# Attention sigmoids kept in PSUM, two kinds of stores moved to SyncE, and a planner that knows of VectorE and GpSimd meeting in SBUF

## The chip, the cores and the metric

The kernel runs on one core of one Trainium2 chip. Such a core has five engines that run side by side, each with its own queue of instructions in fixed order: TensorE (PE in the profile) for matmuls and transposes, VectorE (DVE), ScalarE (ACT), GpSimd (POOL), and SyncE (SP), which here only issues DMAs. They meet through semaphores. Data lies in HBM, in the on-chip memory SBUF, or in PSUM, where TensorE writes its results.

The metric is the device time of one execution in microseconds (us), as the median of several runs. Lower is better. The three runs of the kernel before took 2428.45, 2426.36 and 2428.19 us, median 2428.19.

## The reference

One layer of a decoder, with 2048 tokens of width 1024, all in float32:

```python
a = rmsnorm(x) * g_pre_mix
u = a @ W_in                  # conv value 512, conv gate 512, q 512, k 512, v 512
conv = silu(layernorm(causal_depthwise_conv31(val * sigmoid(gate)) + b))
attn = rmsnorm_per_head(stick_breaking(q, k, v))      # 8 heads of 64
h = x + rmsnorm(concat(conv, attn) @ W_out)
f = (silu(n @ W_gate) * (n @ W_up)) @ W_down          # n = rmsnorm(h), inner width 2816
out = h + rmsnorm(f)
```

Stick-breaking attention has no softmax. With z = q.k / 8, token t gives key s (s < t) the weight sigmoid(z_ts) times the product of 1 - sigmoid(z_tj) over the keys j between s and t. Since 1 - sigmoid(z) = sigmoid(-z), the products are a running product of sigmoid(-z) from the newest key to the oldest.

## The kernel before, in words

**Number format.** A float32 operand is split into a high part H, rounded by ScalarE's copy, and a rest L, made by a subtraction on VectorE or GpSimd. Three matmuls (L x H, H x H, H x L) make one product. The tokens are cut into four groups of 512, and almost every matmul has 512 columns.

**The mixer** is the first half. For each group of tokens it has the input projection (`inproj`, L598 to L602), the convolution on VectorE as 31 taps on a PSUM tile (`taps`, L824), the attention (`attn`) and the output projection (`outproj`, L1041 to L1043). Attention goes head by head (8), chunk by chunk of 512 keys from the newest to the oldest, and in four steps of 128 queries in each. One step of `scores` is: two matmuls write the tile `z` in PSUM (L908, L909; the tile has two buffers), ScalarE writes the sigmoid into an SBUF tile `om` (L911; eight buffers), and VectorE scans `om` in place, from right to left (L914 or L916). A scan is a running product. A diagonal chunk (L914; 128, 256, 384 or 512 wide) adds the mask `lower` and multiplies on; any other chunk (L916, 512 wide) multiplies only, and its second operand does no arithmetic: it is one element of `z`, repeated, except in the later four heads of the last group (`late`), where it is the SBUF constant `one`. There are 320 steps: 128 diagonal ones, 144 with `z` as the operand and 48 with `one`. `values` then transposes the weights (L934), splits them (TH on ScalarE at L590, TL on VectorE at L591) and multiplies them with V (L939, L940). TensorE's results of the input projection go to two PSUM banks (`bank`): for the value columns VectorE multiplies with `sg`, the sigmoid of the gate (L768, L773); for v there are four transposes (L786), whose result is split into two tiles `vt`.

**The feed-forward part** is the second half: a seven-product scheme after Strassen and Winograd. Sums of weight blocks are made on GpSimd ahead of time, in the mixer's shadow (`sums`, L1189). Two steps of it also run beside the mixer: `c11` (88 results) and `p4` (22), each 128x512, which ScalarE copies from PSUM (L1146, L1175) and which are stored in HBM by a DMA that ScalarE itself issues (L1111). `five` computes the other products of the up and gate projections (`b` at L1105; weights split at L1394 and L1395), and the end of the function computes the down projection (`dps` at L1105; operands split at L1622 to L1625, results scaled and added at L1635 and L1654).

**The order.** All instructions are first written in one plausible order, by a list of stages (`PLAN`) and due times. Then `Graph` takes them all, makes the dependencies, and lays them out in time by a list scheduler: `forward` runs a model of the five queues, in which `cost` prices every instruction (busy time, and the later moment at which its result can be used), DMAs have constant prices (`ISSUE`, `LAND`), and buffers are handed out as they come free; `backward` makes the priorities from the reversed program. `arrange` does this 12 times and keeps the order with the earliest end, by the model. `in_order` then ties every engine's instructions in that order. So the order on the chip is fixed when the program is built, and `cost` shapes all of it. On SP, too, a DMA that waits holds up those behind it.

In `cost`, a VectorE operation has one price if an operand is in PSUM and a longer one if all are in SBUF: for 512 elements, with n = 512, a scan 2.04 n + 125 or + 240 ns, a scalar_tensor_tensor 1.04 n + 108 or + 370, a tensor_tensor 1.04 n + 60 or + 500. GpSimd's two-operand operations cost 2.36 n + 125 (products 2.0 n + 125). What the two engines do at the same moment has no bearing on either.

Of the kernel before, what the change touches and what calls it, by code (L numbers as in the profile page):

```python
# [19 lines left out]
P = 128  # L20
# [5 lines left out]
NH = 8  # L26
# [128 lines left out]
def width(a):  # L155
    n = 1
    for _, c in a.ap[1:]:
        n *= int(c)
    return n
# [33 lines left out]
def cost(i, kind, eng, ins, outs):  # L193

    n = width(outs[0])
    if kind == "InstMatmult":
        if size_of(ins[0].dtype) == 4 and not str(ins[0].dtype).endswith("r"):
            return 109, 270
        b = max(width(ins[0]) * 0.443, 109)
        return b, b + 165  # L200
    src = [place(a) for a in ins]
    if eng == "Activation":
        b = n * 0.833 + (49 if src[0] == "PSUM" else 94) + (93 if len(ins) > 1 else 0)
        return b, b + 115
    near = "PSUM" in src or place(outs[0]) == "PSUM"
    if eng == "DVE":
        if kind == "InstTensorScalarPtr":
            if i.is_tensor_tensor_scan:
                b = 2.04 * n + (125 if near else 240)
            elif i.is_scalar_tensor_tensor:  # L210
                b = 1.04 * n + (108 if near else 370)
            else:
                b = 1.04 * n + 160 if place(outs[0]) == "PSUM" else 0.73 * n + 113
        elif kind == "InstBNStatsAggregate":
            b = 93
        elif kind in ("InstTensorReduce", "InstBNStats"):
            b = 1.04 * width(ins[0]) + 48
        elif kind == "InstTensorTensor":
            b = 1.04 * n + (60 if near else 500)
        else:  # L220
            b = n + 100
        return b, b + 100
    if kind == "InstTensorTensor":
        b = 426 + 148 * n if n < 16 else (2.0 if "mult" in str(i.op) else 2.36) * n + 125
    else:
        b = 172 if n == 1 else 280
    return b, b + 65


class Op:  # L230
    def __init__(self, n, ins, eng, dma, busy, late, size):
        self.n, self.ins, self.eng, self.dma = n, ins, eng, dma
        self.busy, self.late, self.size = busy, late, size
        self.after, self.behind, self.tiles = set(), set(), set()


class Graph:


    def __init__(self, insts):  # L240
        self.ops, self.root, self.order, self.users = [], {}, {}, {}
        seen = {}
        for i in insts:
            kind = type(i).__name__
            ins = [a for a in i.ins if hasattr(a, "bass_ap")]
            outs = [a for a in i.outs if hasattr(a, "bass_ap")]
            if not outs:
                continue
            eng, dma = str(i.engine).split(".")[-1], kind == "InstDMACopy"
            busy, late = (ISSUE, 0) if dma else cost(i, kind, eng, ins, outs)  # L250
            o = Op(len(self.ops), i, eng, dma, busy, late, width(outs[0]) * int(outs[0].ap[0][1]) * 4)
            uses = [(a.bass_ap.tensor, box(a), place(a), w) for aps, w in ((ins, False), (outs, True)) for a in aps
                    if hasattr(a.bass_ap.tensor, "tag_meta")]
            for t, b, sp, w in uses:
                if sp != "DRAM" and t.name not in o.tiles:
                    o.tiles.add(t.name)
                    self.users.setdefault(t.name, []).append(o.n)
                    if t.name not in self.root:
                        self.root[t.name] = t
                        self.order.setdefault(t.tag, []).append(t.name)  # L260
                writes, reads = seen.setdefault(t.name, ([], []))
                for old, lst in ((True, writes), (False, reads if w else ())):
                    for q, c, wrote in lst:
                        if sp == "PSUM" or meet(b, c):
                            same = q.eng == eng and not q.dma
                            (o.behind if same and (eng == "PE" or not (old and wrote)) else o.after).add(q.n)
            for t, b, sp, w in uses:
                writes, reads = seen[t.name]
                if sp == "PSUM":
                    writes[:] = [e for e in writes if e[0].eng != eng] + [(o, b, w)]  # L270
                elif w:
                    writes[:] = [e for e in writes if not holds(b, e[1])] + [(o, b, True)]
                    reads[:] = [e for e in reads if not holds(b, e[1])]
                else:
                    reads.append((o, b, False))
            o.behind -= o.after
            self.ops.append(o)
# [32 lines left out]
    def forward(self, ops, prio, slots=True):  # L310
# [18 lines left out]
        busy = dict.fromkeys(ready, 0.0)  # L329
        start, stop = [None] * len(ops), [0.0] * len(ops)  # L330
        moved, flight = 0.0, []
        ev = [(0.0, 0, 0, ())]
        for o in ops:
            if not need[o.n]:
# [28 lines left out]
        while ev:  # L363
# [24 lines left out]
            while look:  # L388
# [5 lines left out]
                while ready[e]:  # L394
# [14 lines left out]
                        moved = max(t + AHEAD, moved) + o.size / RATE  # L409
                        stop[n] = moved + LAND  # L410
                    else:
                        stop[n] = t + o.late
                    heapq.heappush(ev, (busy[e], 1, n, tuple(iss[n])))
                    for lag, then in fin[n].items():
                        heapq.heappush(ev, (stop[n] + lag, 2, n, tuple(then)))
# [8 lines left out]
    def backward(self, start, stop, came):  # L424

        N = len(self.ops)
        rev = [Op(N - 1 - o.n, None, o.eng, o.dma, o.busy, o.late, o.size) for o in self.ops]
        for o in self.ops:
            for p in o.after:
                rev[p].after.add(N - 1 - o.n)  # L430
# [49 lines left out]
def layer_kernel(ctx: ExitStack, tc: tile.TileContext, x, xT, g_pre_mix, w_in, conv_w, conv_b, ln_g, ln_b,  # L480
# [398 lines left out]
    def attn(g):  # L879
# [20 lines left out]
        def scores(u, j):  # L900
# [2 lines left out]
            w = (j + 1) * P if diag else G  # L903
            K = u["K"]
            z = pp.tile([P, G], F32, tag="z", name="z")
            late = g == NG - 1 and u["h"] >= NH // 2
            js = slice(j * P, (j + 1) * P)
            nc.tensor.matmul(z[:, 0:w], hd_["QL"][:, js], K[:, 0:w], start=True, stop=False)  # L908
            nc.tensor.matmul(z[:, 0:w], hd_["QH"][:, js], K[:, 0:w], start=False, stop=True)  # L909
            om = ap.tile([P, G], F32, tag="om", name="om", bufs=NOM)  # L910
            nc.scalar.activation(om[:, 0:w], z[:, 0:w], AF.Sigmoid, scale=-0.125)  # L911
            r = om[:, 0:w][:, ::-1]
            if diag:
                nc.vector.tensor_tensor_scan(r, lower[:, G - w:G][:, ::-1], r, hd_["prev"][j], ALU.add, ALU.mult)  # L914
            else:
                nc.vector.tensor_tensor_scan(r, r, (one if late else z[:, 0:1]).to_broadcast([P, w]), hd_["prev"][j],  # L916
                                             ALU.mult, ALU.bypass)
            hd_["prev"][j] = om[:, 0:1]
            if w == P and g:
                hd_["prev"][j] = sp.tile([P, 1], F32, tag="pv", name="pv", bufs=2)  # L920
# [185 lines left out]

    stored = {}

    def store(t, *key, eng=nc.sync):
        stored[key] = dp.tile([P, *t.shape[1:]], F32, name="_".join(str(k) for k in key))  # L1110
        eng.dma_start(stored[key], t)  # L1111

    def part(t, k, n, *key, eng=nc.sync):

        if key not in stored:
            stored[key] = dp.tile([P, n, G], F32, name="_".join(str(k) for k in key))
        eng.dma_start(stored[key][:, k, :], t)

    fx = {}

# [9 lines left out]
    def c11(g):  # L1130
# [5 lines left out]
        for j in range(HF):  # L1136
            ws = [wts.next() for _ in W]
            pss = [bank("c11") for _ in W]
            for hf in range(2):
                for i, ((WH, WL), ps) in enumerate(zip(ws, pss)):  # L1140
# [3 lines left out]
                            matmul(ps, a[:, kc], b[hf][:, k, :], start=hf == k == 0 and a is WL, stop=last)  # L1144
                    c = next(cs)
                    nc.scalar.activation(c, ps, AF.Copy)  # L1146
                    store(c, "c11", g, i, j, hf, eng=nc.scalar)
                    yield 0.5

    def sums_split(HL, k, t, eng=nc.gpsimd):  # L1150
# [10 lines left out]
    def p4(g):  # L1161
# [4 lines left out]
        for j in range(HF):  # L1166
            for i in range(2):
# [5 lines left out]
                        matmul(ps, a[:, kc], b[0][:, k, :], start=k == 0 and a is WL, stop=last)  # L1173
                c = ev("p4")
                nc.scalar.activation(c, ps, AF.Copy)  # L1175
                store(c, "p4", g, i, j, eng=nc.scalar)
                yield 1

    def sums():
# [609 lines left out]
```

## Time and profile before

| | |
|---|---|
| median of three runs | 2428.19 us (2426.36 to 2428.45) |
| the profiled execution | 2422.51 us, of which its span (first to last instruction) 2420.7 us |
| TensorE busy | 2352.3 us, 97% |
| VectorE busy | 1788.4 us, 74% |
| GpSimd busy | 1207.5 us, 50% |
| ScalarE busy | 1166.5 us, 48% |
| DMA | 656.66 MB, mean 271 GB/s |

All views below are of that one execution, and times in them count from the start of its span. A line of a group reads: line of the code, engine, operation, output<-inputs by the program's names, sizes, count | busy us in all, mean ns of one | us that the engine was idle just before such instructions, and who ended most of it. A line of the waits reads: who waited <- for whom: us in total, times, longest us. A line of the timeline reads: start us, duration us, engine, line, operation, output<-inputs, count, with the idle time before it and who ended it in brackets. A line of a stretch gives each engine's busy us with its count of instructions, then the clock granted to TensorE (1.00 is full), the busy share of the DMA engines and GB/s. PEld is TensorE's loading of weights, which runs beside its matmuls; SPq and ACTq are DMA issues on the queues of SyncE and ScalarE.

### The profile page before, as it was taken

Reading aid. Unit: us, or ns where it says so; the run is one execution under the profiler, and the core shown is the slowest. Engines: PE = TensorE matmul, PEld = TensorE weight load, DVE = VectorE, ACT = ScalarE, POOL = GpSimd, SP = SyncE. Lnnn points to the kernel's source line nnn. Section 1 sums busy time; section 2 is a strip of 40 time slices with the busy share of each in tenths; the row PEclk is TensorE's granted clock in tenths of the full one; section 3 lists DMA queues with packets and bytes.
Section 4 is the critical chain, followed back from the end, with each engine's and each line's share of the span. In section 5 each row is a group of like instructions: output and inputs, shape, how many; then the busy total and the mean of one; then the engine's idle time right before and its main releaser. Section 6 shows DMA issues by size and latency. Waiting matters only on the chain. (4 is left out here: it accounts for less than half of the span.)

```text
span 2420.7 us, 33652 instructions
## 1 busy us (share of the span) xinstructions
PE 2352.3 (97%) x11156; PEld 1929.5 (80%) x11156; DVE 1788.4 (74%) x2177; ACT 1166.5 (48%) x2078; POOL 1207.5 (50%) x994
## 2 busy tenths in 40 slices
PE   7999999999999999999999999999999999999997
PEld 5778887788787878888788887878888888887886
DVE  6997899899998799956842267888766664567556
ACT  4346555474655555455555554334322335454543
POOL 5463235522425234436620047678886445477556
PEclk9999999999999999999999999999999999999998
DMA  9889887897788899987798767999998667658664
GB/s 313 273 260 322 260 252 233 275 317 250 249 276 303 272 308 323 332 292 254 261 316 295 255 233 276 309 311 319 348 336 299 198 236 232 199 189 324 193 193 163
DMA packets 283789, 656.66 MB, mean 271 GB/s; under 512 B 34912, under 2 KB 35424, under 8 KB 283616
## 3 DMA queue, kind: packets, MB, share of 16 engines
q1 hardware_dynamic: 267776, 625.68, 77.6%
q10 hardware_dynamic: 15840, 28.84, 3.1%
q8 instruction: 88, 1.44, 0.2%
q14 instruction: 85, 0.70, 0.1%
HBM read 460.40 MB, written 193.99 MB: 270 GB/s over the span
## 5 line engine op out<-in xcount | busy, mean ns | idle before, releaser
L824 DVE SCALAR_TENSOR_TENSOR cv<-glu,cw,cv 128x512 f32<-128x512 f32 x464 | 345.9, 746 | 6.4
L1395 POOL TENSOR_TENSOR wL<-raw,wH 128x512 fp32r<-128x512 f32 x176 | 264.9, 1529 | 169.9 <-ACT wH L1394 169.7
L1625 DVE TENSOR_TENSOR xL__20078<-t__20080,xH__20077 128x512 fp32r<-128x512 f32 x154 | 197.5, 1288 | 150.3 <-ACT xH__20077 L1624 148.9
L1623 POOL TENSOR_TENSOR xL__20076<-t__20079,xH__20075 128x512 fp32r<-128x512 f32 x154 | 212.5, 1385 | 159.4 <-ACT xH__20075 L1622 155.2
L591 DVE TENSOR_TENSOR TL<-at,TH 128x512 fp32r<-128x512 f32 (+1 forms) x320 | 188.6, 597 | 132.8 <-ACT TH L590 126.7
L598 PE MATMUL inps<-xH,wL 128*128 128x512 f32 x640 | 259.7, 407 | 12.4 <-ACT sg L768 11.7
L602 PE MATMUL inps<-xL,wH 128*128 128x512 f32 x640 | 255.3, 400 | 0.5 <-DVE xL L738 0.5
L600 PE MATMUL inps<-xH,wH 128*128 128x512 f32 x640 | 255.7, 400 | 0.0
L1105 PE MATMUL dps<-xH__20075,xL__20078 128*128 128x512 f32 x616 | 241.6, 392 | 5.6 <-DVE xL__20078 L1625 5.6
L1105 PE MATMUL dps<-xH__20075,xH__20077 128*128 128x512 f32 x616 | 240.8, 391 | 0.0
L1105 PE MATMUL dps<-xL__20076,xH__20077 128*128 128x512 f32 x616 | 239.4, 391 | 0.0
L590 ACT ACTIVATE TH<-at 128x512 fp32r<-128x512 f32 (+1 forms) x320 | 168.8, 536 | 122.8 <-PE at L934 114.2
L552 ACT ACTIVATE wH<-raw 128x1024 fp32r<-128x1024 f32 x156 | 165.8, 1063 | 127.6 <-PE inps L602 57.0
L911 ACT ACTIVATE om<-z 128x512 f32<-128x512 f32 (+2 forms) x320 | 168.4, 540 | 88.9 <-PE z L909 87.3
L556 POOL TENSOR_TENSOR wL<-raw,wH 128x1024 fp32r<-128x1024 f32 x50 | 122.1, 2443 | 163.7 <-ACT wH L552 149.4
L934 PE MATMUL at<-idr,om 128*128 128x128 f32 x1088 | 184.2, 273 | 6.0 <-DVE om L914 3.0
L1622 ACT ACTIVATE xH__20075<-t__20079 128x512 fp32r<-128x512 f32 x154 | 97.1, 630 | 192.7 <-POOL xL__20076 L1623 141.5
L1189 POOL TENSOR_TENSOR sum<-sum 128x512 f32<-128x512 f32 x88 | 126.7, 1440 | 117.9 <-DMA sum<-in_w_up_dram 45.0
L1394 ACT ACTIVATE wH<-raw 128x512 fp32r<-128x512 f32 x176 | 101.4, 624 | 155.9 <-PE b L1105 58.3
L934 PEld LDWEIGHTS at<-idr,om 128*128 128x128 f32 x1088 | 137.1, 140 | 46.2 <-DVE om L914 5.8
L916 DVE TENSOR_TENSOR_SCAN om<-om,z 128x512 f32<-128x512 f32 x124 | 156.8, 1268 | 3.9 <-ACT om L911 3.7
L598 PEld LDWEIGHTS inps<-xH,wL 128*128 128x128 f32 x640 | 121.5, 190 | 37.8 <-ACT sg L768 8.3
(296 smaller groups left out, 6120.7 us busy)
## 6 DMA issues: line engine op xcount, KB each, us to landing
wL<-wL SPq DMA_DIRECT2D x156, 512.0 KB, 5.3
raw<-in_w_in_dram SPq DMA_DIRECT2D x80, 512.0 KB, 6.0
t__20080<-u SPq DMA_DIRECT2D x154, 256.0 KB, 3.0
c<-c ACTq DMA_DIRECT2D x88, 256.0 KB, 5.4
t__20079<-wd SPq DMA_DIRECT2D x88, 256.0 KB, 2.6
K<-kd SPq DMA_DIRECT2D x80, 256.0 KB, 4.9
V<-vd SPq DMA_DIRECT2D x80, 256.0 KB, 4.6
u<-accf SPq DMA_DIRECT2D x22, 768.0 KB, 5.7
```

What stands on the lines that cost most here:

```text
L590: nc.scalar.activation(H, ps, AF.Copy)
L591: nc.vector.tensor_tensor(L, ps, H.bitcast(F32), ALU.subtract)
L598: nc.tensor.matmul(ps, WL[:, kc], aH[t](k), start=k == 0, stop=False)
L600: nc.tensor.matmul(ps, WH[:, kc], aH[t](k), start=False, stop=False)
L602: nc.tensor.matmul(ps, WH[:, kc], aL[t](k), start=False, stop=k == KT - 1)
L824: nc.vector.scalar_tensor_tensor(to, gl[c][:, k:k + G], cw[:, c, k:k + 1], a, ALU.mult, ALU.add)
L911: nc.scalar.activation(om[:, 0:w], z[:, 0:w], AF.Sigmoid, scale=-0.125)
L934: nc.tensor.transpose(pt[:, j * P:(j + 1) * P], u["A"][j][:, b * P:(b + 1) * P], id32)
L1105: return nc.tensor.matmul(ps, a, b, skip_group_check=True, **flags)
L1395: nc.gpsimd.tensor_tensor(l, t, f32(h), sub)
L1623: nc.gpsimd.tensor_tensor(WL, w, f32(WH), sub)
L1625: nc.vector.tensor_tensor(UL, t, f32(UH), sub)
```

## The change

Three things are changed.

1. ScalarE writes the sigmoid back into the PSUM tile `z`; `om` is written by the scan alone. The scan reads `z` from right to left and writes `om`. The second operand of the scans that are not diagonal is always the SBUF constant `one`; the case `late` is gone.
2. The stores of the c11 and p4 results are issued by SP.
3. The planner's prices: VectorE's longer prices for operations with all operands in SBUF are gone. `both_in_sbuf` marks VectorE and GpSimd operations with two inputs at least 128 wide and all operands in SBUF. When, in `forward`, such a VectorE operation starts while a marked GpSimd operation runs, or any GpSimd operation starts while a marked VectorE operation runs, the new one gets longer (`more`) and the running one may (`push`), by shares of what is left of the running one and of the new one's own time. GpSimd's own prices change as well, to 2.35 n + 35 for operations of 16 elements and more.

```diff
@@ cost
-    near = "PSUM" in src or place(outs[0]) == "PSUM"
     if eng == "DVE":
         if kind == "InstTensorScalarPtr":
             if i.is_tensor_tensor_scan:
-                b = 2.04 * n + (125 if near else 240)
+                b = 2.04 * n + 125
             elif i.is_scalar_tensor_tensor:
-                b = 1.04 * n + (108 if near else 370)
+                b = 1.04 * n + 108
...
         elif kind == "InstTensorTensor":
-            b = 1.04 * n + (60 if near else 500)
+            b = 1.04 * n + 60
...
-    if kind == "InstTensorTensor":
-        b = 426 + 148 * n if n < 16 else (2.0 if "mult" in str(i.op) else 2.36) * n + 125
+    if kind == "InstTensorTensor" and n >= 16:
+        b = 2.35 * n + 35
+    elif "pow" in str(getattr(i, "op", "")):
+        b = 375 + 150 * n
     else:
-        b = 172 if n == 1 else 280
+        b = 125 if n < 16 else 215
     return b, b + 65
 
+def both_in_sbuf(i, ins, outs):
+
+    return sum(width(a) >= 128 for a in ins) > 1 and all(place(a) == "SB" for a in ins + outs)
@@ Graph.forward
-                        stop[n] = t + o.late
+                        more = 0.0
+                        if o.wide if e == "DVE" else e == "Pool":
+                            other = "Pool" if e == "DVE" else "DVE"
+                            m, rest = runs.get(other), busy.get(other, 0.0) - t
+                            if m is not None and rest > 0 and ops[m].wide:
+                                if e == "DVE":
+                                    more, push = min(1.2 * o.busy, 0.55 * rest), 0.28 * min(rest, 2 * o.busy)
+                                elif o.wide:
+                                    push = min(1.2 * rest, 0.55 * o.busy)
+                                    more = 0.28 * (rest + push)
+                                else:
+                                    more, push = 0.8 * rest, 0.0
+                                busy[e] += more
+                                busy[other] += push
+                                heapq.heappush(ev, (busy[other], 1, m, ()))
+                        runs[e] = n
+                        stop[n] = t + o.late + more
@@ attn, scores
-            late = g == NG - 1 and u["h"] >= NH // 2
...
-            nc.scalar.activation(om[:, 0:w], z[:, 0:w], AF.Sigmoid, scale=-0.125)
-            r = om[:, 0:w][:, ::-1]
+            nc.scalar.activation(z[:, 0:w], z[:, 0:w], AF.Sigmoid, scale=-0.125)
+            r, zr = (t[:, 0:w][:, ::-1] for t in (om, z))
             if diag:
-                nc.vector.tensor_tensor_scan(r, lower[:, G - w:G][:, ::-1], r, hd_["prev"][j], ALU.add, ALU.mult)
+                nc.vector.tensor_tensor_scan(r, lower[:, G - w:G][:, ::-1], zr, hd_["prev"][j], ALU.add, ALU.mult)
             else:
-                nc.vector.tensor_tensor_scan(r, r, (one if late else z[:, 0:1]).to_broadcast([P, w]), hd_["prev"][j],
-                                             ALU.mult, ALU.bypass)
+                nc.vector.tensor_tensor_scan(r, zr, one.to_broadcast([P, w]), hd_["prev"][j], ALU.mult,
+                                             ALU.bypass)
@@ c11
-                    store(c, "c11", g, i, j, hf, eng=nc.scalar)
+                    store(c, "c11", g, i, j, hf)
@@ p4
-                store(c, "p4", g, i, j, eng=nc.scalar)
+                store(c, "p4", g, i, j)
```

Left out here: the bookkeeping of the mark (`wide`) in `Op`, `Graph` and `backward`, and the `eng` argument of `store` and `part`, which is gone.

More of the change, by code (lines that the diff above doesn't have):

```diff
@@ L222, in cost, with __init__ @@
         return b, b + 100
-    if kind == "InstTensorTensor":
-        b = 426 + 148 * n if n < 16 else (2.0 if "mult" in str(i.op) else 2.36) * n + 125
+    if kind == "InstTensorTensor" and n >= 16:
+        b = 2.35 * n + 35
+    elif "pow" in str(getattr(i, "op", "")):
+        b = 375 + 150 * n
     else:
-        b = 172 if n == 1 else 280
+        b = 125 if n < 16 else 215
     return b, b + 65
+def both_in_sbuf(i, ins, outs):
+    return sum(width(a) >= 128 for a in ins) > 1 and all(place(a) == "SB" for a in ins + outs)
 class Op:
-    def __init__(self, n, ins, eng, dma, busy, late, size):
-        self.n, self.ins, self.eng, self.dma = n, ins, eng, dma
+    def __init__(self, n, ins, eng, dma, busy, late, size, wide):
+        self.n, self.ins, self.eng, self.dma, self.wide = n, ins, eng, dma, wide
         self.busy, self.late, self.size = busy, late, size
@@ L250, in __init__ @@
             busy, late = (ISSUE, 0) if dma else cost(i, kind, eng, ins, outs)
-            o = Op(len(self.ops), i, eng, dma, busy, late, width(outs[0]) * int(outs[0].ap[0][1]) * 4)
+            o = Op(len(self.ops), i, eng, dma, busy, late, width(outs[0]) * int(outs[0].ap[0][1]) * 4,
+                   eng in ("DVE", "Pool") and not dma and both_in_sbuf(i, ins, outs))
             uses = [(a.bass_ap.tensor, box(a), place(a), w) for aps, w in ((ins, False), (outs, True)) for a in aps
@@ L331, in forward @@
         moved, flight = 0.0, []
+        runs = {}
         ev = [(0.0, 0, 0, ())]
@@ L426, in backward @@
         N = len(self.ops)
-        rev = [Op(N - 1 - o.n, None, o.eng, o.dma, o.busy, o.late, o.size) for o in self.ops]
+        rev = [Op(N - 1 - o.n, None, o.eng, o.dma, o.busy, o.late, o.size, o.wide) for o in self.ops]
         for o in self.ops:
@@ L1107, in layer_kernel, with store, part @@
     stored = {}
-    def store(t, *key, eng=nc.sync):
+    def store(t, *key):
         stored[key] = dp.tile([P, *t.shape[1:]], F32, name="_".join(str(k) for k in key))
-        eng.dma_start(stored[key], t)
-    def part(t, k, n, *key, eng=nc.sync):
+        nc.sync.dma_start(stored[key], t)
+    def part(t, k, n, *key):
         if key not in stored:
             stored[key] = dp.tile([P, n, G], F32, name="_".join(str(k) for k in key))
-        eng.dma_start(stored[key][:, k, :], t)
+        nc.sync.dma_start(stored[key][:, k, :], t)
     fx = {}
```

## The prediction

> **What bounds the kernel now.** I read the page's busy line first, then the busy times by stretch with the granted clock, then the waits of TensorE, then one of those waits in order of time, and last VectorE's groups by shape.
>
> ```profile
> PE 2352.3 (97%) x11156; PEld 1929.5 (80%) x11156; DVE 1788.4 (74%) x2177; ACT 1166.5 (48%) x2078; POOL 1207.5 (50%) x994
> ```
>
> ```profile
> core 0: 2420.7 us, clock 0.995
> ```
>
> TensorE is busy for 2352.3 of 2420.7 us, so it sat idle for 68.4. The mean granted clock of 0.995 takes another 0.005 x 2420.7 = 12.1 us. No matmul is added or removed, so about 80 us is all that the whole change can work on, and a part of it is fixed.
>
> ```profile
> core 0: us, PE busy (x) PEld busy (x) DVE busy (x) ACT busy (x) POOL busy (x), PEclk, DMA share, GB/s
> 0.00:100.00 100.00, 81.93 (x371) 66.14 (x372) 72.23 (x98) 42.79 (x70) 50.96 (x58) 0.98 0.91 288
> 400.00:500.00 100.00, 91.95 (x437) 74.06 (x436) 91.27 (x123) 50.49 (x86) 50.57 (x60) 0.97 0.80 277
> 500.00:700.00 200.00, 197.30 (x1010) 160.99 (x1008) 196.77 (x269) 112.44 (x206) 61.01 (x63) 1.00 0.79 260
> 1440.00:2400.00 960.00, 946.43 (x4165) 777.59 (x4164) 634.89 (x651) 386.84 (x695) 644.06 (x466) 1.00 0.77 260
> 1700.00:1800.00 100.00, 100.00 (x442) 82.59 (x441) 66.47 (x76) 31.77 (x55) 82.71 (x58) 1.00 0.97 347
> 2400.00:2421.00 21.00, 11.57 (x41) 9.06 (x41) 11.80 (x18) 2.89 (x8) 5.46 (x8) 0.74 0.30 125
> ```
>
> Two regimes show. From 1700 to 1800 TensorE is never idle (442 matmuls in 100 us): nothing off TensorE matters there. In the mixer (attention, convolution taps and input projection together, up to about 1400) VectorE is nearly as full as TensorE: 196.77 of 200 us between 500 and 700, 91.27 of 100 between 400 and 500. There a late VectorE instruction soon makes TensorE late, and the two stretches with idle TensorE, 0 to 100 and 400 to 500, also have the granted clock down at 0.98 and 0.97.
>
> ```profile
> PE inps L598 <- ACT sg L768: 11.7, 6, 5.0
> PE tps L608 <- DVE xrow L684: 10.6, 4, 7.4
> PE dps L1105 <- DVE xL__20078 L1625: 5.6, 6, 3.2
> PE b L1105 <- POOL wL L1395: 5.1, 2, 3.0
> PE o L940 <- DVE TL L591: 4.2, 7, 1.5
> PE o L939 <- ACT TH L590: 3.0, 2, 2.6
> PE at L934 <- DVE om L914: 3.0, 5, 1.0
> PE b L1105 <- DVE glu L1402: 2.2, 3, 1.6
> PE z L908 <- DVE om L916: 1.9, 5, 0.5
> ```
>
> The columns are us in total, times, longest. The longest wait in the mixer's middle, is read in two rows, ScalarE's and TensorE's:
>
> ```profile
> 466.28 0.38 ACT L590 ACTIVATE vt<-vps 128x256 fp32r<-128x256 f32 x1 [2.13 <-DVE vt L591]
> ```
>
> ```profile
> 467.20 0.79 PE L598 MATMUL inps<-xH,wL 128*128 128x512 f32 x1 [5.00 <-ACT sg L768]
> ```
>
> TensorE stands 5.00 us for ScalarE's sg, but ScalarE itself stood 2.13 us for VectorE's vt. So the wait put down to ScalarE is VectorE behind its planned place. Fixed: the first 10.6 us (tps, loading x), and what lies after 2400 (21 - 11.57 = 9.4 us idle, and 0.26 x 21 = 5.5 us of clock). That leaves 80 - 10.6 - 9.4 - 5.5 = about 55 us that an order could win.
>
> **Part 1, sigmoids in PSUM.** No instruction is added; operands move. The scans at L914 and half of the last group's at L916 read and write SBUF only; the others already have one PSUM operand.
>
> ```profile
> L916 DVE TENSOR_TENSOR_SCAN om<-om,z 128x512 f32<-128x512 f32 x124 | 156.8, 1268 | 3.9 <-ACT om L911 3.7
> ...
> L916 DVE TENSOR_TENSOR_SCAN om<-om,one 128x512 f32<-128x512 f32 x44 | 64.7, 1481 | 24.9 <-ACT om L911 24.9
> L914 DVE TENSOR_TENSOR_SCAN om<-lower,om 128x512 f32<-128x512 f32 x32 | 50.9, 1590 | 2.2 <-ACT om L911 2.2
> L914 DVE TENSOR_TENSOR_SCAN om<-lower,om 128x384 f32<-128x384 f32 x32 | 39.8, 1244 | 3.1 <-ACT om L911 3.1
> ...
> L914 DVE TENSOR_TENSOR_SCAN om<-lower,om 128x256 f32<-128x256 f32 x32 | 26.2, 817 | 0.8 <-ACT om L911 0.7
> L914 DVE TENSOR_TENSOR_SCAN om<-lower,om 128x128 f32<-128x128 f32 x32 | 17.6, 551 | 8.6 <-ACT om L911 8.5
> ```
>
> The groups of the stretch from 1280 to 1370, where GpSimd does almost nothing, have the second group again:
>
> ```profile
> L916 DVE TENSOR_TENSOR_SCAN om<-om,one 128x512 f32<-128x512 f32 x11 | 14.0, 1279 | 11.9 <-ACT om L911 11.9
> ```
>
> There an SBUF-only scan by itself takes 1279 ns, as long as one with a PSUM operand (1268). So the excess of the SBUF-only rows is GpSimd's doing, and I price the new scans at 1268 for 512 wide and the narrower ones on the planner's old line for a scan beside PSUM, 2.04 n + 125 + 100 ns, which gives that 1268 (as 1269): 1008, 747 and 486. Diagonal scans: 32 x ((1590 - 1268) + (1244 - 1008) + (817 - 747) + (551 - 486)) = 32 x 693 = 22.2 us. Late scans: 44 x (1481 - 1268) = 9.4 us. VectorE gives up some 32 us, and GpSimd's partners in those collisions get shorter too. Of this only what makes TensorE less late counts. The mixer waits behind VectorE are 11.7 + 4.2 + 3.0 + 3.0 + 1.9 = 23.8 us, and the clock lost in two of their stretches is 2 + 3 (0.98 and 0.97 of 100 us), 29 together. The relief is spread over the whole mixer, a fraction of a us at each scan, and the taps around the scans stay, so it shortens waits more than it ends them. I take a quarter: **-7 us**, with 0 and -18 as ends.
>
> [...]
>
> ScalarE's sigmoid now writes PSUM, which no ScalarE row shows. The nearest rows are VectorE's with either output, 698 against 686:
>
> ```profile
> L1402 DVE TENSOR_TENSOR accf<-b,accf 128x512 f32<-128x512 f32 x53 | 36.3, 686 | 23.5 <-PE b L1105 22.1
> L1402 DVE TENSOR_TENSOR b<-b,accf 128x512 f32<-128x512 f32 x44 | 30.7, 698 | 46.4 <-PE b L1105 46.1
> ```
>
> 320 x 12 ns either way is 4 us of an engine half idle in the mixer: 0. What is added is a hold: z (two buffers) is now kept until the scan ends in 176 of 320 steps, where the sigmoid used to free it. The other 144 hold it so already, and TensorE waited 1.9 us for them in all. At that rate the 176 cost 176 / 144 x 1.9 = 2.3 us, part of it beside waits that are there anyway: **+1**, ends 0 and +2.3; its bad case is a rival.
>
> **Part 2, stores from SP.** 2 x 11 x 2 x 2 = 88 c11 stores and 11 x 2 = 22 p4 stores (groups, j, weights, halves) leave ScalarE's queue.
>
> ```profile
> 1284.92 0.33 ACTq L1111 DMA_DIRECT2D c<-c  x1
> ```
>
> ```profile
> SPq L554 <- PE c L1105: 66.2, 22, 8.1
> ```
>
> 110 x 0.33 = 36 us of issue time goes off ScalarE and onto SP. ScalarE is half idle there, and of TensorE's waits on it only L939's 2.6 us could lie there: 0 to -2. On SP a store stands behind nothing but blocks what follows it: it waits for ScalarE's copy, and the loads of weights, K and V queue behind. But SP already stands 66.2 us in 22 places for a free weight buffer in c11, by the second line, so those loads have lead; 0 to +4, by a wait or two like the longest above. Sum **0**. The cover is that lead; without it, each late load costs TensorE what it lacks.
>
> **Part 3, the planner's costs.** It fixes the order of all engines, so every queue may change. Before, a VectorE operation with all operands in SBUF had one long price; now it has a short one, plus shares where GpSimd runs at once. What the trace says of that:
>
> ```profile
> 2384.03 0.68 DVE L1625 TENSOR_TENSOR xL__20078<-t__20080,xH__20077 128x512 fp32r<-128x512 f32 x1
> ...
> 2396.52 1.74 DVE L1625 TENSOR_TENSOR xL__20078<-t__20080,xH__20077 128x512 fp32r<-128x512 f32 x1
> ```
>
> ```profile
> 2388.18 1.29 POOL L1623 TENSOR_TENSOR xL__20076<-t__20079,xH__20075 128x512 fp32r<-128x512 f32 x1
> ...
> 2394.79 4.61 POOL L1623 TENSOR_TENSOR xL__20076<-t__20079,xH__20075 128x512 fp32r<-128x512 f32 x3
> ```
>
> The same VectorE operation takes 0.68 or, beside GpSimd's three, 1.74, so one price is wrong both ways, by 0.45 and 0.6 (1.04 x 512 + 500 + 100 = 1132 ns in the old formula), and the new shape is the right one. In the feed-forward part (13.6 us of idle TensorE from 1440 to 2400) its waits on such operations are 5.6 + 5.1 + 2.2 = 12.9 us. A better order takes part of them: **-4 us** (a third); the rest of the order's change is chance, which I hold at 0 with +-8.
>
> [...] But a GpSimd operation took 1.29 alone and 4.61 / 3 = 1.54 beside VectorE's, and VectorE's grew as well: both give way, so the trace bears the shares out.
>
> **Sum.** -7 + 1 + 0 - 4 = **-10 us**. The profiled execution took 2422.5 us, 1.8 more than its span; the median of the three runs is 2428.2, 5.7 above it. I carry the difference over to the median: 2428.2 - 10 = **2418 us**. A measurement of this kernel can tell about 0.2%, 4.9 us, from no change.
>
> **The rivals.** (a) No change: 2428, within 4.9 us. A new order trades one wait for another; where TensorE is full (1700 to 1800) collisions of VectorE and GpSimd cost nothing today, so a planner that knows of them wins nothing. Against it: VectorE's 32 us are real, and partly where it is 91 to 98% full.
>
> (b) Slower: the z buffers. TensorE writes the next scores only when the scan two steps back has ended, so any backlog on VectorE reaches TensorE through z. Price: where one tap stands ahead of the scan, TensorE loses up to its length:
>
> ```profile
> L824 DVE SCALAR_TENSOR_TENSOR cv<-glu,cw,cv 128x512 f32<-128x512 f32 x464 | 345.9, 746 | 6.4
> ```
>
> It decides from 10 / 0.75 = 13 of the 176 steps on. If one in five is hit, 35 x 0.75 = 26 us: 2428 - 10 + 26 = 2444. For it: the taps fill VectorE to 98% there. Against: the 144 steps with the same hold lost 1.9 us together.
>
> (c) The planner gets much better: VectorE's waits nearly vanish from the mixer and half the feed-forward's: -29 - 6 = -35, 2393. Against it: the planner still prices every DMA by constants, and the first stretch keeps its start.
>
> **How the numbers follow.** The forecast, faster by 5 to 30 us, has 0.54; (c) 0.05; (a) 0.20; (b) and other losses of the new order 0.21. So faster 0.59, same 0.20, slower 0.21. The range goes from -29 (-18 for part 1, +1 for z, -4 for part 3, -8 by the order) to +12 (part 1 at 0, z +2, SP +4, part 3 at -2, +8 by the order), 2399 to 2440; outside it lie (c) and half of (b) with the other losses, about 0.15. Within the forecast alone it is 2399 to 2423.
>
> **What would show it.** Right: L914's 512-wide row near 1270 and L916 in one group of 168 near 1270; VectorE's busy time down by 25 to 40 us; TensorE's idle time down to about 58; the waits on sg and TL shorter; no 0.97 in a stretch of the mixer. Part 2: SP's waits on ScalarE's c copies appear, TensorE's waits for weights do not. Wrong: a wait of z on the scans far above 1.9 us (b), or idle TensorE near 68 us with the waits at new places (a). [...]

## The result and the profile after

The changed kernel takes 2398.26 us (median of four runs, 2396.89 to 2399.50), the kernel before 2427.97 beside it: a ratio of 0.9879, with 0.9862 to 0.9896 as its interval. That is 29.4 us less by the ratio, where 10 were forecast, and just outside the range. The profiled execution has a span of 2397.7 us against 2420.7. That difference is 23 us only, because the profiled execution of before lay 5.5 us below its median. Executions differ by their clock: those of before were granted 0.991 to 0.995 in the mean, mostly 0.993, the profiled one 0.995; those of the changed kernel 0.995 to 0.997. So sizes below come from ratios of medians, and the traces say where.

First the page's busy line and the span with the mean clock.

```profile
PE 2345.4 (98%) x11156; PEld 1930.4 (81%) x11156; DVE 1762.9 (74%) x2177; ACT 1167.3 (49%) x2078; POOL 1170.7 (49%) x994
```

```profile
core 0: 2397.7 us, clock 0.996
```

TensorE is idle for 2397.7 - 2345.4 = 52.3 us instead of 68.4. VectorE works 25.5 us less, and GpSimd, of which no instruction was touched, 36.8 us less. The waits of TensorE after:

```profile
PE tps L632 <- DVE xrow L708: 10.4, 4, 7.3
PE inps L622 <- ACT sg L792: 8.5, 4, 4.7
PE o L963 <- DVE TL L615: 8.2, 9, 2.3
PE dps L1128 <- DVE xL__20078 L1648: 2.9, 2, 2.0
PE at L957 <- DVE om L939: 2.5, 4, 1.2
PE b L1128 <- POOL wL L1418: 2.3, 2, 1.5
PE b L1128 <- DVE accf L1425: 2.0, 4, 1.3
...
PE z L931 <- DVE om L939: 0.7, 2, 0.4
...
PE b L1128 <- DVE glu L1425: 0.6, 1, 0.6
```

The wait on the fixed start is unchanged. Shorter are sg (11.7 to 8.5), and in the feed-forward part xL, wL and glu (5.6, 5.1 and 2.2 to 2.9, 2.3 and 0.6). Longer is o on TL (4.2 to 8.2). The wait of z on the scans, by which rival (b) would have shown, is 0.7 us. The scans, by shape:

```profile
L939 DVE TENSOR_TENSOR_SCAN om<-z,om,one 128x512 f32<-128x512 f32 x168 | 213.2, 1276 | 49.4 <-ACT z L934 48.1 <-PE at L957 1.0
L937 DVE TENSOR_TENSOR_SCAN om<-lower,z 128x512 f32<-128x512 f32 x32 | 40.6, 1268 | 3.7 <-ACT z L934 3.7
L937 DVE TENSOR_TENSOR_SCAN om<-lower,z 128x384 f32<-128x384 f32 x32 | 32.2, 1006 | 1.5 <-ACT z L934 1.4
...
L937 DVE TENSOR_TENSOR_SCAN om<-lower,z 128x256 f32<-128x256 f32 x32 | 23.6, 739 | 1.8 <-ACT z L934 1.7
L937 DVE TENSOR_TENSOR_SCAN om<-lower,z 128x128 f32<-128x128 f32 x32 | 15.2, 475 | 13.4 <-ACT z L934 13.4
```

These are the forecast durations (1268, 1008, 747, 486) within 11 ns. The late scans' 1481 went to 1276. On SP, its waits on ScalarE's copies have appeared, and in exchange it stands less for a free weight buffer of c11 (34.6 us, 66.2 before); none of it reaches TensorE's list of waits:

```profile
SPq L1134 <- ACT c L1169: 65.6, 57, 3.0
...
SPq L578 <- PE c L1128: 34.6, 22, 4.7
```

### The profile page after: what moved, and what is told of

Read it like the earlier page. It is cut to its first block, busy times and chain, and to the rows that moved or that the text cites. A ratio compares the mean times of both kernels' runs of the same rounds, so it can differ in the third digit from the quotient of the medians.

```text
span 2397.7 us, 33860 instructions
## 1 busy us (share of the span) xinstructions
PE 2345.4 (98%) x11156; PEld 1930.4 (81%) x11156; DVE 1762.9 (74%) x2177; ACT 1167.3 (49%) x2078; POOL 1170.7 (49%) x994
## 4 chain that ended last, share of the span: by engine, by line
PE 79%; DVE 13%; issue 3%; POOL 2%; DMA 2%; ACT 1%; SPq 0%; DVEq 0%; POOLq 0%; ACTq 0%
PE b L1128 17%; PE dps L1128 17%; PE c L1128 8%; PE inps L622 5%; PE inps L624 5%; PE inps L626 5%; DVE cv L848 4%; PE at L957 4%; PE p L1128 2%; PE o L963 2%; PE z L931 2%; PE ops L1065 2%; PE ops L1064 2%; PE z L932 2%; PE ops L1066 2%
## 5 line engine op out<-in xcount | busy, mean ns | idle before, releaser
L1648 DVE TENSOR_TENSOR xL__20078<-t__20080,xH__20077 128x512 fp32r<-128x512 f32 x154 | 196.5, 1279 | 146.8 <-ACT xH__20077 L1647 146.7
L939 DVE TENSOR_TENSOR_SCAN om<-z,om,one 128x512 f32<-128x512 f32 x168 | 213.2, 1276 | 49.4 <-ACT z L934 48.1
L934 ACT ACTIVATE z<-z 128x512 f32<-128x512 f32 (+2 forms) x320 | 167.0, 528 | 115.3 <-PE z L932 112.9
L576 ACT ACTIVATE wH<-raw 128x1024 fp32r<-128x1024 f32 x156 | 165.1, 1060 | 119.1 <-PE inps L626 59.7
L1212 POOL TENSOR_TENSOR sum<-sum 128x512 f32<-128x512 f32 x88 | 117.1, 1330 | 98.5 <-DMA sum<-in_w_up_dram 48.8
L622 PEld LDWEIGHTS inps<-xH,wL 128*128 128x128 f32 x640 | 121.5, 190 | 32.8 <-issue 5.5
```

The source lines that it names most:

```text
L622: nc.tensor.matmul(ps, WL[:, kc], aH[t](k), start=k == 0, stop=False)
L939: nc.vector.tensor_tensor_scan(r, zr, one.to_broadcast([P, w]), hd_["prev"][j], ALU.mult, ALU.bypass)
L1648: nc.vector.tensor_tensor(UL, t, f32(UH), sub)
```

## The experiments

Every run has the kernel before beside it, which took 2426.9, 2426.2, 2425.4, 2426.8 and 2423.2 us in the five sets of runs. "Saved" is 1 - ratio, times 2427 us.

| run | median us | ratio (interval) | saved us |
|---|---|---|---|
| a_only: part 1 | 2411.26 | 0.9941 (0.9928 to 0.9954) | 14.3 |
| b_only: part 2 | 2432.89 | 1.0025 (1.0016 to 1.0034) | -6.1 |
| c_only: part 3 | 2416.90 | 0.9964 (0.9950 to 0.9977) | 8.7 |
| a_and_c | 2392.66 | 0.9862 (0.9848 to 0.9875) | 33.5 |
| ac_again, the same again | 2393.39 | 0.9875 (0.9861 to 0.9889) | 30.3 |
| ac_hop61, redrawn | 2392.87 | 0.9858 (0.9839 to 0.9878) | 34.5 |
| before_hop61, redrawn | 2422.31 | 0.9983 (0.9973 to 0.9993) | 4.1 |
| after_again | 2397.60 | 0.9883 (0.9869 to 0.9896) | 28.4 |
| after_hop61, redrawn | 2393.60 | 0.9867 (0.9854 to 0.9880) | 32.3 |
| sp_in_ac_order | 2395.68 | 0.9883 (0.9871 to 0.9896) | 28.4 |
| ac_no_shares | 2440.45 | 1.0058 (1.0043 to 1.0072) | -14.1 |
| order_of_ac_sbuf | 2424.54 | 0.9990 (0.9979 to 1.0001) | 2.4 |
| before_29_taps | 2441.90 | 1.0074 (1.0060 to 1.0089) | -18.0 |
| taps_29_paced | 2427.54 | 1.0002 (0.9993 to 1.0012) | -0.5 |
| ac_with_32us | 2404.38 | 0.9916 (0.9904 to 0.9928) | 20.4 |
| ac_with_34us_uneven | 2406.66 | 0.9923 (0.9911 to 0.9936) | 18.7 |
| ac_with_lumps | 2411.33 | 0.9947 (0.9934 to 0.9960) | 12.9 |
| ac_late_sbuf | 2400.61 | 0.9897 (0.9881 to 0.9913) | 25.0 |

The theory at the start was the prediction's: part 1 shortens VectorE's work and a share of that reaches TensorE. The rivals were that part 3 or the redrawn order is what pays, or that part 2 is.

### The parts by themselves

a_only has the change of `scores`, b_only that of the stores, c_only that of `cost` and `Graph`; a_and_c is the changed kernel with its stores back on ScalarE's queue (p4's in the same way, left out here):

```diff
@@ a_and_c, against the changed kernel
-                    store(c, "c11", g, i, j, hf)
+                    store(c, "c11", g, i, j, hf, eng=nc.scalar)
...
```

> Only the sigmoids stay in PSUM (scans read z and write om); stores and planner's costs as before. The order is planned anew. Theory 1 (scans without GpSimd's share relieve VectorE): 2418 to 2423, VectorE's busy time down by about 32 us. Theory 2 (the planner's costs carry the gain): 2423 to 2428. Theory 3 (any new order is a draw of +-8 us): anywhere from 2415 to 2435. L914 at 512 wide near 1270 ns in all three.

> Only the c11 and p4 stores are issued by SP. Theory 1 and 2: 2426 to 2430, nothing to see. Rival (ScalarE's issue time held TensorE up from 880 to 1390): 2418 or less, with the gain inside that stretch. Theory 3: 2420 to 2436.

> Only the planner's costs are changed; every instruction is as before, in another order. Theory 1: -4, 2424. Theory 2: most of the 30 us, 2403 to 2410, with TensorE's waits on VectorE's and GpSimd's splits in the feed-forward part down from 13 us to below 6. Theory 3: 2420 to 2436.

> Sigmoids in PSUM and the planner's costs, stores from ScalarE as before. Theories 1 and 2: as the full change, 2396 to 2402. Rival of the stores: 2405 or more.

Parts 1 and 3 save 14.3 and 8.7 alone, and 30.3 to 34.5 together: some 10 us more than their sum. Part 2 alone loses 6.1. a_only and a_and_c are faster than any theory had them, c_only lies between the ranges, and b_only is in the range of the third theory alone. Two stretches, one in the mixer and one in the feed-forward part, show where; each fence holds one kernel's: before, a_only, c_only, a_and_c.

```profile
100.00:500.00 400.00, 384.69 (x1968) 315.83 (x1967) 362.70 (x515) 217.41 (x399) 181.33 (x185) 0.99 0.84 275
...
1440.00:2360.00 920.00, 909.70 (x4009) 748.15 (x4009) 609.35 (x627) 368.84 (x661) 612.80 (x441) 1.00 0.78 263
```

```profile
100.00:500.00 400.00, 390.13 (x2001) 320.15 (x2000) 366.65 (x524) 221.98 (x407) 174.41 (x184) 1.00 0.83 276
...
1440.00:2360.00 920.00, 910.61 (x4006) 748.78 (x4005) 607.27 (x620) 368.46 (x661) 607.78 (x436) 1.00 0.78 263
```

```profile
100.00:500.00 400.00, 386.66 (x1953) 315.99 (x1952) 362.59 (x513) 219.35 (x395) 183.82 (x182) 0.98 0.82 270
...
1440.00:2360.00 920.00, 914.52 (x4038) 753.95 (x4037) 618.38 (x631) 372.63 (x668) 619.25 (x444) 1.00 0.78 265
```

```profile
100.00:500.00 400.00, 393.16 (x2039) 325.44 (x2037) 363.54 (x527) 231.16 (x422) 175.94 (x190) 1.00 0.85 279
...
800.00:1300.00 500.00, 492.36 (x2454) 404.47 (x2453) 353.97 (x448) 273.07 (x478) 178.88 (x147) 1.00 0.88 299
1440.00:2360.00 920.00, 916.33 (x4046) 755.50 (x4045) 607.54 (x627) 374.69 (x675) 615.46 (x444) 1.00 0.78 264
```

In the feed-forward stretch TensorE's busy time goes up with part 3 alone (909.70 to 914.52), not with part 1 (910.61). In the mixer part 1 brings more (390.13) than part 3 (386.66), and both bring 393.16. Over the 384.69 of before that is 5.4 and 2.0 alone and 8.5 together, near the sum: the 10 us more are not in this stretch. The busy lines of a_only, with a span of 2412.4 us, and of c_only, with 2415.1, show where they are:

```profile
PE 2353.6 (98%) x11156; PEld 1932.5 (80%) x11156; DVE 1757.8 (73%) x2177; ACT 1168.1 (48%) x2078; POOL 1171.9 (49%) x994
```

```profile
PE 2355.4 (98%) x11156; PEld 1932.1 (80%) x11156; DVE 1794.7 (74%) x2177; ACT 1167.8 (48%) x2078; POOL 1203.4 (50%) x994
```

TensorE is idle for 58.8 and 59.7 us in them, and for 2393.0 - 2345.7 = 47.3 in a_and_c (its line stands further below): 9.6 and 8.7 less than before alone, 21.1 together, again near the sum. Its busy time, for as many instructions, goes up by 1.3 and 3.1 alone and down by 6.6 together, and the clock goes with it: 0.993 and 0.993 in these two traces, 0.996 in a_and_c's. Over all their executions the mean clock is 0.993 for before, 0.994 and 0.993 for the parts alone and 0.996 for both; 0.003 x 2427 = 7 us. So most of the extra is granted clock. What made the clock higher with both was not tested.

### How much is the draw of the order

A constant of the planner was moved a little, for another order of equal standing.

```diff
-HOP = 60.0
+HOP = 61.0
```

> The kernel before with the planner's hop at 61 ns in place of 60. Theories 1 and 2: 2424 to 2430. Theory 3: 2418 to 2436; if it lies near 2415, the kernel before was an unlucky draw and part of the gain is that.

> Sigmoids in PSUM and the new costs, stores from ScalarE, and the planner's constant for a hop between engines 61 ns in place of 60: no cost is changed in earnest, the order is drawn anew. Theories 1 and 2: 2390 to 2396 as without it. Theory 3 (each order is a draw of +-8 us): 2385 to 2402.

> Sigmoids in PSUM and the new costs, stores from ScalarE, once more beside these: 2390 to 2395.

> The changed kernel once more, beside the others: 2396 to 2400.

> The changed kernel with the planner's hop at 61 ns in place of 60, a neutral new drawing of its order. If the stores on SP cost 5 us whatever the order: 2396 to 2400. If the 5 us are the draw: 2390 to 2395 is as likely.

These redraws moved the time by 4 us at most, half of the 8 that the prediction allowed, and the four orders that the new planner made of parts 1 and 3, with part 2 or without, all save 28 us or more. So 30 us are no draw. An order of the old planner can still be a worse draw than that: b_only loses 6.1 us and before_29_taps, further below, 18.0. The 4 us between a_and_c and the changed kernel may be one: after its redraw the changed kernel (0.9867) is level with a_and_c (0.9862 and 0.9875).

### Part 2, at one order

The changed kernel's instructions, stores on SP, were run in the order that the planner gave a_and_c, kept as a table of start times:

```diff
-    mixer.arrange()
+    mixer.start = planned()
```

> The changed kernel's instructions in the order that the planner made with the stores on ScalarE, written out as a table: SP gets the 110 stores at the places where ScalarE had them. If SP's queue itself costs the 5 to 6 us that the stores' move shows: 2397 or more. If that is the drawing of a new order: 2390 to 2395.

It saves 28.4 against 30.3 to 34.5, with overlapping intervals for ac_again: SP's stores cost 0 to some 4 us. The 6.1 us of b_only have another cause, which its timelines show, of GpSimd, VectorE and TensorE in turn:

```profile
397.92 9.90 POOL L711 TENSOR_TENSOR xcol<-xcol,rb 128x512 f32<-128x512 f32 x8
407.78 2.93 POOL L1189 TENSOR_TENSOR sum<-sum 128x512 f32<-128x512 f32 x2
```

```profile
398.67 10.91 DVE L872 TENSOR_TENSOR xL<-ma,xH 128x512 fp32r<-128x512 f32 x1
```

```profile
410.90 0.79 PE L940 MATMUL o<-TL,V 128*128 128x512 f32 x1 [9.13 <-DVE TL L591]
```

One VectorE instruction with both operands in SBUF, 0.68 us long by itself, took 10.91 us, while GpSimd ran eight two-operand instructions one after the other at 9.90 / 8 = 1.24 us each, none of them lengthened, and went on with a ninth at once; it ended half a us behind the ninth. TensorE lost 9.13 us by it. The products right behind this wait mostly took 0.63 us each, those before it 0.39 or 0.40. In before's trace products of 0.63 us stand where the granted clock is 0.50 (467 to 472, right behind the wait of 5.00 us), those of 0.39 where it is 1.00 (450 to 460): by that the clock suffered here as well. So, by this trace, b_only's loss is one bad meeting of VectorE and GpSimd in a redrawn order, not a store that SP delays.

### Collisions taken out and put back at the same order

order_of_ac_sbuf takes a_and_c's order and issues the instructions of before in it. All 320 sigmoids go to SBUF again, but only 176 scans then have SBUF operands alone; the other 144 read one element of z in PSUM, as before, and are no slower for it:

```profile
L1123 DVE TENSOR_TENSOR_SCAN om<-om,z 128x512 f32<-128x512 f32 x124 | 156.9, 1268 | 12.0 <-ACT om L1118 12.0
```

> Every instruction is that of the kernel before (sigmoids in SBUF, the scans as before), but all engines' orders are those that the planner made for sigmoids in PSUM with the new costs, written out as a table. Theory 1 (what counts is that the scans are shorter on the chip): about 2412 to 2418, that is the 34 us less what the sigmoids' move gave alone (15 to 24). Theory 2 (what counts is the order): 2395 to 2400, the collisions of the SBUF-only scans cost little once the order is right. L914 at 512 wide above 1500 ns in both.

It saves 2.4 us where a_and_c saves 30.3 to 34.5: at one order the collisions cost about 30 us, more than either theory had. The two busy lines, a_and_c first:

```profile
PE 2345.7 (98%) x11156; PEld 1930.3 (81%) x11156; DVE 1755.2 (73%) x2177; ACT 1168.0 (49%) x2078; POOL 1170.9 (49%) x994
```

```profile
PE 2352.0 (97%) x11156; PEld 1929.3 (80%) x11156; DVE 1794.5 (74%) x2177; ACT 1166.6 (48%) x2078; POOL 1203.6 (50%) x994
```

VectorE gets 39.3 us longer and GpSimd 32.7. The stretches of order_of_ac_sbuf:

```profile
100.00:500.00 400.00, 382.42 (x1952) 313.82 (x1951) 363.48 (x509) 216.52 (x393) 181.18 (x181) 1.00 0.82 268
...
800.00:1300.00 500.00, 485.37 (x2414) 395.58 (x2413) 377.11 (x454) 270.47 (x477) 203.65 (x153) 1.00 0.86 292
1440.00:2360.00 920.00, 916.36 (x4047) 755.65 (x4046) 615.69 (x634) 377.53 (x676) 623.26 (x446) 1.00 0.78 264
```

The mixer loses 393.16 - 382.42 = 10.7 us of TensorE in the first of them and 492.36 - 485.37 = 7.0 in the second, the feed-forward part nothing. What a collision is, its timelines show, VectorE's first:

```profile
1175.28 3.43 DVE L1123 TENSOR_TENSOR_SCAN om<-om,one 128x512 f32<-128x512 f32 x2
...
1238.18 2.35 DVE L1123 TENSOR_TENSOR_SCAN om<-om,one 128x512 f32<-128x512 f32 x1
```

```profile
1175.40 2.22 POOL L776 TENSOR_TENSOR wL<-raw,wH 128x512 fp32r<-128x512 f32 x1
1177.59 2.20 POOL L1396 TENSOR_TENSOR sum<-sum 128x512 f32<-128x512 f32 x1
...
1238.17 1.28 POOL L1396 TENSOR_TENSOR sum<-sum 128x512 f32<-128x512 f32 x1 [1.90 <-DMA sum<-in_w_up_dram]
```

At 1238.17 GpSimd starts a hundredth of a us earlier and takes its 1.28 us as if alone, to 1239.45. The scan, 1.27 us alone, ends at 1240.53, which is 1.08 us later, nearly its whole length: it was blocked until GpSimd had ended. From 1175.28 the two scans take 3.43 us in all and the two GpSimd instructions 2.22 and 2.20 instead of 1.29: here each blocks the next of the other in turn. Worked out from the whole trace: of the 80 SBUF-only scans of 512, 22 were lengthened, and all 22 ended 1.078 to 1.087 us after the GpSimd instruction that stood before them. In before's trace it is 25 of 80, of which 24 ended 1.077 to 1.088 us after it and one 1.139; the other 55 took 1286 ns at most.

### What a us of VectorE's time is worth

Does that loss count by its length? Two taps of the convolution were left out (the conv output lacks them), in before_29_taps with the generator's pace changed by that, in taps_29_paced with the pace kept:

```diff
@@ taps_29_paced, against before
             for k in range(1, CW):
+                if k < 3:
+                    yield 1
+                    continue
```

> The kernel before without two of the 31 taps (k = 1 and 2 are left out, so the convolution is another one): 32 operations of 746 ns, 24 us of VectorE's time in PSUM that never meets GpSimd. If a us of VectorE in the mixer is worth a us of the kernel: 2402 to 2406. If a quarter, as the prediction took it: 2418 to 2422. If regular time costs nothing and only irregular durations do: 2424 to 2428.

> As the kernel without two of the 31 taps (k = 1 and 2 left out), but the generator yields once in place of each tap that is missing, so that taps, attention and projections are written out in the pace of the kernel before. If the loss of the first such kernel was its pace: now 2426 or less. If a us of regular VectorE time is worth a third of a us, as the 32 us given back showed: 2415 to 2422. If it is worth one: 2400 to 2406.

The first missed: the new pace gave another order, with a meeting like b_only's (the same kind of instruction stood for 6.96 us, at 416.6), and it lost 18.0 us. With the pace kept, VectorE's 345.9 - 322.9 = 23 us of taps gained nothing. The order was planned anew, so a few us of draw are in this too; but taking away regular work that the plan knows of brought nothing to be seen. The other way, time was added to a_and_c behind the same 176 scans, with results that nothing uses. ac_with_32us was planned anew with that; the other two runs keep its order and read other numbers of columns:

```diff
+            if diag or g == NG - 1 and u["h"] >= NH // 2:
+                nc.vector.tensor_reduce(dummy, om[:, 0:P], AX.X, ALU.add)
```

> Sigmoids in PSUM and the new costs, stores from ScalarE, and after each of the 176 scans that were SBUF-only before one more VectorE operation, a row sum of 128 columns of om that nobody reads, planned at 181 ns: 32 us of VectorE's time are given back, but with a fixed duration. If the 32 us of VectorE's time were the gain: 2415 to 2425. If the irregular durations were: 2392 to 2400.

> The kernel with one more VectorE operation after each of 176 scans, in exactly its order (as a table), but the operations are uneven and other than planned: 44 of them read 512 columns of om and 132 read 16, about 34 us in all against 32. If VectorE's time alone counts: 2403 to 2406. If durations that the plan does not know cost by themselves: 2412 or more.

> Parts 1 and 3 in the order of ac_with_32us, with the same 176 extra operations of VectorE behind the scans (a reduction over columns of om, whose result nothing uses), but 15 of them read 3 x 512 columns (lumps of about 1.65 us, as long as the longest collisions of a scan) and the other 161 read 16 columns, some 35 us in all. If it is VectorE's lumps, unknown to the plan, that make collisions cost as much as they last: 2415 or more. If VectorE's time counts by its sum, whatever its shape: 2403 to 2407, as ac_with_32us (2404.4) and ac_with_34us_uneven (2406.7); then the rest of the 31 us of collisions comes by way of GpSimd's own lengthening.

The added rows, of ac_with_32us and of ac_with_lumps:

```profile
L943 DVE TENSOR_REDUCE dummy<-om 128x1 f32<-128x128 f32 x176 | 48.4, 275 | 1.5
```

```profile
L1158 DVE TENSOR_REDUCE dummy<-om 128x3 f32<-128x1536 f32 x15 | 26.1, 1740 | 0.0
L1160 DVE TENSOR_REDUCE dummy<-om 128x1 f32<-128x16 f32 x161 | 25.7, 159 | 1.4
```

Against the mean of a_and_c's two runs and its redraw (32.8 saved), evenly spread time costs 12.4 us, uneven time 14.1, which the intervals don't tell apart, and time with 15 lumps of 1.74 us 19.9. VectorE's busy time goes up by 35.1 us in the first (1790.3 - 1755.2) and by 39.5 in the last (1794.7), as by the collisions' 39.3, which cost 30. So time with lumps costs two thirds of that. The first and the last of these runs fall between their expectations: the last 10 us are not VectorE's length in lumps alone. GpSimd's 32.7 us of lengthening, or the places of the lumps, could be them; that stays open.

ac_late_sbuf puts only the 48 late scans back in SBUF, in a_and_c's order.

> Instructions and order of a_and_c, with only the 48 late scans back in SBUF (ScalarE writes their sigmoid into om, the scan works in place); the 128 diagonal ones keep their input in PSUM. With all 176 back in SBUF this order took 31 us more. If each scan counts by the time that it loses, as the prediction's 9.4 of 31.6 us has it: about 2402. If the late scans, which run where GpSimd is fullest, carry it: 2410 or more. If the diagonal ones do: 2393 to 2397.

It loses 32.8 - 25.0 = 7.8 us of the 30, a quarter, where the prediction's lengths gave 9.4 of 31.6. The loss is where they run:

```profile
800.00:1300.00 500.00, 487.78 (x2429) 398.26 (x2428) 365.31 (x449) 270.62 (x475) 193.75 (x147) 1.00 0.87 296
```

TensorE has 492.36 - 487.78 = 4.6 us less there than in a_and_c. By difference, some 22 us are then the diagonal scans', if the two add up.

### Are the planner's shares needed

ac_no_shares keeps the new short prices and takes the shares away:

```diff
-                   eng in ("DVE", "Pool") and not dma and both_in_sbuf(i, ins, outs))
+                   False)
```

> Sigmoids in PSUM, stores from ScalarE, and the new prices without the shares for VectorE and GpSimd meeting in SBUF (nothing is marked). If the shares are what the planner gains by: 2405 to 2415, no better than the sigmoids alone (2411). If the new prices do it without them: 2390 to 2396.

It loses 14.1 us, 47 more than a_and_c, and is far slower than either expectation. Its first two waits of TensorE:

```profile
PE b L1128 <- DVE accf L1425: 14.1, 8, 2.7
PE b L1128 <- DVE glu L1425: 10.9, 5, 6.1
```

Those are the feed-forward part's products waiting for VectorE's sums. Short prices alone would have been a loss; part 3 needs the shares.

## Why the prediction came out too small

**The bound was read rightly.** TensorE's idle time and clock were what the change could work on, the mixer behind VectorE held most of it, and the fixed start is still there (10.4 us). The tail was taken as fixed and was not quite: the xL wait there halved.

**Part 1: the step that failed.** The durations (1268, 1008, 747, 486 ns), VectorE's 25 to 40 us less and GpSimd's partners getting shorter came out as put. The conversion did not: "I take a quarter", -7 us. The runs show 14.3 alone, and 30.3 - 8.7 to 34.5 - 8.7, 22 to 26, on top of part 3, outside even the ends of 0 and -18. The quarter is not far off for regular VectorE time: 0 of 23 us for the taps, 12.4 of 35 for the even additions. But the excess of 1590 - 1268 was not 0.32 us in each scan. It was a mean over scans that lost nothing and scans that stood up to a whole GpSimd instruction: in before's trace 21 of these 32 scans took 1251 to 1284 ns and the other 11 took 1570 to 2752. At one order such time cost 0.76 us at the end per us of VectorE (30 / 39.3).

**The sum of the parts.** This is the second step that failed: the prediction added independent terms, and gave part 3 the feed-forward waits only, with chance in the mixer. Alone the three give 14.3 + 8.7 - 6.1 = 17 us, inside the range. Together they give 29. Of the 10 us between parts 1 and 3 some 7 are granted clock, of which the prediction counted 5, among the waits that part 1 works on; it is the clock that the carried difference, below, is about. That a plan pays more when nothing collides behind its back fits c_only: it planned with collisions still there and saved 8.7, and the same instructions in an order planned without them 2.4. It was not tested by itself.

**Part 3** was mis-sized in the same direction: -4 against 8.7. In c_only's trace the feed-forward waits on xL, wL and glu are 2.9 + 2.3 + 0.6 = 5.8 us, so 7 of the 12.9 went, not a third. Rival (c), the better planner, was half right. The prediction held that "both give way" and that the trace so bore the shares out; its 4.61 / 3 = 1.54 us was a mean as well, of 1.26, 1.71 and 1.72. In the runs' traces one engine stood until the other had ended: the 22 scans that end some 1.08 us behind GpSimd's instruction, and the instruction that took 10.91 us behind nine. Both engines got longer because each lost in turn (from 1175.28 on, 3.43 us for two scans, 2.22 and 2.20 for two GpSimd instructions). Even so, shares of what is left of the running instruction were a usable mean of such blocking: without them the kernel loses 47 us. A planner that prices the blocking itself was not tried.

**The 512-wide scans from PSUM** took 1268 and 1276 ns in the mean, as the SBUF scan with GpSimd quiet did (1279), now with all 512 elements from PSUM.

**Part 2 and the z buffers** came out as put: 0 to some 4 us, and 0.7 us of z waits. With c11's stores on SP no wait for a transfer stands in TensorE's list. a_and_c, with them on ScalarE, is the quickest by its median, but the redrawn changed kernel is level with it.

**The clock.** "No 0.97 in a stretch" held by a hair, with TensorE 6 us busier than before in the same stretch:

```profile
400.00:500.00 100.00, 97.96 (x482) 79.93 (x481) 92.10 (x129) 54.66 (x94) 45.49 (x58) 0.98 0.83 280
```

**The carried difference.** The prediction carried the 5.7 us between the profiled execution and the median over to the new kernel. But they are 0.002 of the clock (0.002 x 2427 = 4.9 us): most executions of before have 0.993, so the clock took 0.007 x 2427 = 17 us from them, not the 12.1 of the profiled one, and the new kernel has 0.996 in the mean. The span fell by 23.0 us and the median by 29.7, so some 6 us of the miss of 20 are this. Behind b_only's wait of 9.13 us the products took 0.63 us, and behind before's of 5.00 us the granted clock was 0.50; behind before's of 3.01 us at 1474.83 they were back at 0.39 with the second. That the new kernel has more clock because it waits less is argued from this and not shown.

## What to carry to other kernels

A row's mean above the lone duration of the same instruction was here no stretch of each instance (in the row of 1590 ns, 21 of 32 scans took 1251 to 1284): look at single instances, and price a collision as these traces show it, as blocking that can last nearly as long as the other engine's instruction (1.08 us of 1.28 at 1238.17), and as long as many of them if those follow one another (10.91 us behind nine). In a program whose order is fixed ahead, take such collisions out by moving one operand to PSUM before any us is saved elsewhere, since here each us of them cost 0.76, twice what a us of evenly added VectorE time did (12.4 / 35.1 = 0.35), and taking 23 us of regular work away brought nothing. Then let the planner price those that remain; here the two paid more together than apart.

## What the runs showed of the hardware

In these traces a VectorE instruction with both inputs in SBUF did not share with a GpSimd two-input instruction: in order_of_ac_sbuf a scan lost up to 1.4 us to one GpSimd instruction (1024 wide, 2.40 us long), and in b_only a 0.68 us subtraction took 10.91 us behind nine, between the first eight of which it did not get in. The scans whose input comes from PSUM were not touched by this, although their other operand and their output are in SBUF: in the changed kernel's trace 63 of the 512-wide scans ran for more than half of their time beside such GpSimd instructions, and none of them took more than 1292 ns. ScalarE's 512-wide sigmoid got no longer by writing to PSUM, 593 ns against 603. The rows are before's and the changed kernel's:

```profile
L911 ACT ACTIVATE om<-z 128x512 f32<-128x512 f32 x224 | 132.7, 603 | 47.1 <-PE z L909 46.1
```

```profile
L934 ACT ACTIVATE z<-z 128x512 f32<-128x512 f32 x224 | 132.0, 593 | 71.3 <-PE z L932 69.7 <-PE o L963 0.6 <-ACT z L934 0.2
```
